# A planning margin, full-shape matmuls and single stores in a hybrid decoder step

## The chip, the cores and the metric

The kernel runs on one core of one Trainium2 chip. The metric is device time in microseconds (us), the median of three runs.

## The reference

One step of a one-layer decoder is computed for a prompt of 512 tokens and for 8 samples of 8 new tokens each, so 576 tokens in all, with model width 1024:

```python
proj = rmsnorm(x, norm1_w) @ w_in        # q, k, v, gate of retention; q, k, v of attention
ro = swish(gate) * groupnorm(retention(q, k, v, state))
ao = dilated_attention(q, k_all, v_all)  # k_all: the cached 1024 rows, then the new rows
x = x + concat([ro, ao]) @ w_out
ua, ub = split(rmsnorm(x, norm2_w) @ w_up)
x = x + (silu(causal_conv3(ua)) * ub) @ w_down
y = rmsnorm(x, normf_w)
```

Beside y, the new retention states, the windows of keys and values (cached rows followed by the new ones) and the convolution states are outputs. All data are 32-bit floats. There are eight retention heads and eight attention heads of 64 columns, handled as four head pairs (hp 0 to 3).

## The kernel before, in words

**Dense matmuls.** Every projection is cut into chunks of 128 output columns. Weights and activations are split into a high and a low part (`whi`, `wlo`; `bhi`, `blo` and others), and a chunk is 48 matmuls of 288 columns (line 254): 8 row blocks, three products, two halves of the 576 tokens. ACT makes `whi`, DVE makes `wlo`, SP loads the raw weights.

**The input projection** (`in_proj`) has 28 chunks. The first 12 feed retention, the next 12 feed attention (for each head pair: keys, queries, values), and the last 4 are the retention gates. While they run, small work is put between them: retention until 149 us, then attention until about 339 us. The output projection, the up and the down projections follow.

**Attention of the prompt** (`attn_unit`, 16 units: a head pair and a block i of 128 queries, whose scores reach over (i+1)*128 keys). For i > 0 the queries are split as well: `qa`, 128 rows high, holds the high part of one head twice, and `ql` holds the low part of both heads, one in its upper and one in its lower 64 partitions. The scores of each head are a full matmul with `qa` (line 764) and a matmul over 64 rows with half of `ql` (line 766). Then come DVE (add the bias, minimum), ACT (exponential), POOL (scale), PE transposes (line 791), copies and the product with the values (line 804).

**Attention of the samples** (`attn_sample`, 8 units: a head pair and four samples). The cached keys are transposed on PE (line 877, `keys`). A unit has scores in four column groups of 32 (line 887), softmax, transposes (lines 910 and 911, the last one only 64 columns wide), two ACT copies and one DVE copy into `spt`, and the product with the values (line 923) in four column groups: six blocks of 128 rows and one of 64 rows, which holds the new tokens.

**natural** transposes new keys and values back to token rows (line 495: four transposes of 128 columns and one of 64). `store_window` writes them out with one DMA for the prompt (line 504) and eight of 4 KB for the samples (line 507).

**The order is planned.** Each stream is a generator. `Merge` keeps a clock in ns, runs the stream that is due, and the order in which they emit is the order of the instructions on every engine. A stream yields a pair (cost, wait): the clock moves on by cost, and the stream is due again wait later. Streams with a work total (`left`: `in_proj`, `attn_prompt`, `attn_sample`) share what time is over; the others go first once they are due. The clock only fixes an order: the hardware waits on semaphores alone. `room(n)` and `give(n)` count the four PSUM tiles `m`. At most two prompt units and two sample units are under way. Two gates matter:

```python
# in_proj: keys, queries, values of hp 2 wait for all six units of hp 0, those of hp 3 for hp 1
while hp > 1 and (sec < 3 and ret_done[0] < hp - 1 or sec > 3 and used.get(hp - 2, 0) < 6):
    yield None
# attn_sample: at most six value tiles are held; the next ones load after a unit's line 923
while len(V) > 5:
    yield None
```

The tables of the functions are these:

Of the kernel before, what the change touches and what calls it, by code (L numbers as in the profile page):

```python
# [11 lines left out]
F32R = mybir.dt.float32r  # L12
# [6 lines left out]
P = 128  # L19
D = 1024  # L20
NP = 512
NS = 64
T = NP + NS
H2 = T // 2
B = 8
TS = 8
PAST = 1024
# [5 lines left out]
KEYS = 768  # L33
SK = KEYS + TS
# [61 lines left out]
class Merge:  # L96
# [6 lines left out]

    def __init__(self):
        self.clock, self.live, self.n = 0.0, [], 0

    def floor(self):
        return min([e["vt"] for e in self.live if e["left"] and not e["stuck"]], default=0.0)
# [6 lines left out]
    def run(self, until=None):  # L115
        while self.live and not (until and until()):
            free = [e for e in self.live if not e["stuck"]]
            assert free, "every stream waits"
            ok = [e for e in free if e["at"] <= self.clock]
            if ok:  # L120
                e = min(ok, key=lambda e: (e["left"] is not None, e["vt"] if e["left"] else e["at"], e["n"]))
            else:
                e = min(free, key=lambda e: (e["at"], e["n"]))
                self.clock = e["at"]
            try:
                c = next(e["g"])
            except StopIteration:
                self.live.remove(e)
                c = (0.0, 0.0)
            if c is None:  # L130
                e["stuck"] = True
                continue
            low = self.floor()
            for x in self.live:
                if x["stuck"]:
                    x["stuck"] = False
                    x["vt"] = max(x["vt"], low)
            self.clock += c[0]
            e["at"] = self.clock + c[1]
            if e["left"]:  # L140
                p = c[2] if len(c) > 2 else c[0]
                e["vt"] += p / e["left"]
                e["left"] = max(e["left"] - p, 2000.0)
# [3 lines left out]
def decoder_step(ctx, tc, a):  # L147
    nc = tc.nc
    pe, dve, act, pool, sp = nc.tensor, nc.vector, nc.scalar, nc.gpsimd, nc.sync
# [10 lines left out]
    held = [0]  # L160

    def room(n):

        while held[0] + n > 4:
            yield None
        held[0] += n

    def give(n):
        held[0] -= n

    def dtile():
        return psd.tile([P, 1024], F32, name="d", tag="d")
# [1 line left out]
    def f32(ap):  # L174
        return ap.bitcast(F32)
# [91 lines left out]
    ident = cst.tile([P, P], F32, name="ident")  # L267
# [27 lines left out]
    def rows_of(j):  # L295
        return (P, slice(j * P, (j + 1) * P)) if j < 4 else (NS, slice(NP, T))
# [31 lines left out]
    mg = Merge()  # L328
# [21 lines left out]
    for nme, n in (("conv_w", 66), ("conv_b", 22), ("norm2_w", 8), ("ret_gn_w", 4), ("ret_gn_b", 4)):  # L350
        src = a[nme]
# [134 lines left out]
    rpx = mid.enter_context(ExitStack())  # L486
    rp = rpx.enter_context(tc.tile_pool(name="ret", bufs=2, reuse_waits="tile"))

    def natural(src, dst):

        yield from room(2)
        p1, p2 = mtile(), mtile()
        for j in range(5):
            r, s = rows_of(j)
            pe.transpose((p1[:, s] if j < 4 else p2[:NS, :P]), src[:, s], ident)  # L495
        yield 550.0, 300.0
        act.copy(dst[:, 0:4], p1.rearrange("p (j c) -> p j c", j=4))
        dve.tensor_copy(dst[:NS, 4], p2[:NS, :P])
        give(2)

    def store_window(nat, which, hp):
        c = slice(hp * P, (hp + 1) * P)
        op_ = a[f"o_w{which}_p"].rearrange("a (j p) h d -> p (a j) (h d)", p=P)[:, :, c]
        sp.dma_start(op_, nat[:, 0:4])
        os_ = a[f"o_w{which}_s"]
        for b in range(B):
            sp.dma_start(os_[b, PAST:PAST + TS].rearrange("t h d -> t (h d)")[:, c], nat[b * TS:(b + 1) * TS, 4])

    copies = []
    for which in "kv":  # L510
# [10 lines left out]
    def in_post(m, ps):  # L521
        sec, hp = m // 4, m % 4
        y = tok(ps)
        if sec == 3:
            t = atp.tile([P, T], F32, name="t3", tag="t6", bufs=1)
            dve.tensor_mul(t, y, rstd_b)
            yield 0.0, 800.0
            act.activation(t, t, AF.Silu)
            yield 0.0, 1700.0
            while ret_done[0] <= hp:  # L530
                yield None
            (dve if hp == 3 else pool).tensor_tensor(roT[:, hp], roT[:, hp], t, op=OP.mult)
            ready.add(hp)
        elif sec < 4:
            while sec == 1 and hp not in kready:
                yield None
            r = R.setdefault(hp, {})
            t = rp.tile([P, T], F32, name=f"r{sec}", tag=f"r{sec}", bufs=2)
            dve.tensor_mul(t, y, kds.pop(hp) if sec == 1 else rstd_b)
            if m in first:  # L540
                evac.append(m)
            while not psm:
                yield None
            yield 0.0, 700.0
            if sec in (1, 2):
                n = rp.tile([P, 5, P], F32, name=f"n{sec}", tag=f"n{sec}", bufs=2)
                yield from natural(t, n)
                r["kv"[sec - 1]] = n
            if sec == 1 and hp < 3:
                mg.add(load_kdec(hp + 1))  # L550
            r[sec] = t
        else:
            r = A.setdefault(hp, {})
            t = atp.tile([P, T], F32, name=f"t{sec}", tag=f"t{sec}", bufs=1 if sec == 6 else 2)
            if sec == 4:
                dve.scalar_tensor_tensor(t, y, -(DH ** -0.5), rstd_b, op0=OP.mult, op1=OP.mult)
                yield 0.0, 2300.0
                for h2, q in halves():
                    pool.tensor_copy(qbs[hp % 2][q, :, h2 * TS:(h2 + 1) * TS],
                                     t[q, NP:].rearrange("p (b t) -> p b t", b=B))  # L560
            else:
                dve.tensor_mul(t, y, rstd_b)
                yield 0.0, 1700.0
                n = atp.tile([P, 5, P], F32, name=f"n{sec}", tag=f"n{sec}", bufs=1 if sec == 5 else 2)
                yield from natural(t, n)
                if sec == 6:
                    r["v"] = n
            r[sec] = t
            if sec > 4:
                yield 0.0, 3100.0  # L570
                store_window(n, "k" if sec == 5 else "v", hp)
# [159 lines left out]


    half, used = {}, {}
    pbs, O, flying = {}, {}, {"p": 0, "s": 0}

    def load_bias(hp):
        for h2 in range(2):
# [3 lines left out]
    def attn_unit(hp, i):  # L741

        n = (i + 1) * P
        S, PT = [], []
        if i:

            q_ = A[hp][4][:, i * P:(i + 1) * P]
            qa = [kvb[0].tile([P, P], F32R, name=f"qa{h2}", tag=f"qa{h2}", bufs=2) for h2 in range(2)]
            ql = kvb[0].tile([P, P], F32R, name="ql", tag="ql", bufs=2)
            for h2, q in halves():  # L750
                act.copy(qa[h2][q], q_[q])
                act.copy(qa[h2][other(h2)], q_[q])
            yield 0.0, 1000.0
            for h2, q in halves():
                dve.tensor_sub(ql[q], q_[q], f32(qa[h2][q]))
            yield 0.0, 500.0
        yield from room(2)
        pss = [mtile() for _ in halves()]
        if i == 0:
            for h2, q in halves():  # L760
                pe.matmul(pss[h2][:, :n], A[hp][4][q, :P], A[hp][5][q, :n], start=True, stop=True)
        else:
            for h2 in range(2):
                pe.matmul(pss[h2][:, :n], qa[h2], kk[hp][h2][:, :n], start=True, stop=False)  # L764
            for h2, q in halves():
                pe.matmul(pss[h2][:, :n], ql[q], kk[hp][h2][q, :n], start=False, stop=True)  # L766
        for ps in pss:
            S.append((ps, atp.tile([P, 512], F32, name="s", tag="s", bufs=4),
                      atp.tile([P, 4], F32, name="sc", tag="sc", bufs=8)))
# [43 lines left out]
                ready.add(4 + hp)  # L813
        flying["p"] -= 1

    kk, scored = {}, {}

    def k_split(hp):

# [10 lines left out]
    def other(h2):  # L830
        return slice(64 - h2 * 64, 128 - h2 * 64)
# [15 lines left out]
    kvb = []  # L847
    SW = SK + NS

    def attn_sample():  # L850
# [31 lines left out]
        def unit(u):  # L882
# [25 lines left out]
            ps = dtile()  # L908
            for j in range(6):
                pe.transpose(ps[:, j * P:(j + 1) * P], s[:, j * P:(j + 1) * P], ident)  # L910
            pe.transpose(ps[:NS, KEYS:KEYS + P], s[:, SK:], ident)
            yield 770.0, 200.0
            pt = kvb[0].tile([P, 7, P], F32, name="spt", tag="spt", bufs=1)
            dve.tensor_copy(pt[:, :3].rearrange("p j q -> p (j q)"), ps[:, :384])
            act.copy(pt[:, 3:6].rearrange("p j q -> p (j q)"), ps[:, 384:KEYS])
            act.copy(pt[:NS, 6], ps[:NS, KEYS:KEYS + P])  # L916
            yield 0.0, 2200.0
            yield from room(1)
            ps = mtile()
            for j in range(7):  # L920
                for x in range(4):
                    n, v = (P, V[u, x][:, j]) if j < 6 else (NS, A[hp]["v"][:NS, 4])
                    pe.matmul(ps[x * 32:(x + 1) * 32, :P], pt[:n, j, x * 32:(x + 1) * 32], v, start=j == 0, stop=j == 6,  # L923
                              tile_position=(0, x * 32))
                if j == 3:
                    yield 900.0, 0.0
# [68 lines left out]
    psm.append(ctx.enter_context(tc.tile_pool(name="psm", bufs=4, space=PSUM, reuse_waits="tile")))  # L995
    mg.run(lambda: fin_ret)
    rpx.close()

    kvx = mid.enter_context(ExitStack())
    kvb.append(kvx.enter_context(tc.tile_pool(name="kv", bufs=2, reuse_waits="tile")))  # L1000

    MIX = [4, 5, 6, 7, 0, 1, 2, 3]

# [8 lines left out]

    mg.add(mix_split())
    mg.run()
    mid.close()


# [306 lines left out]
```

## Time and profile before

| | |
|---|---|
| median of three runs | 831.99 us (831.43 to 834.12) |
| profiled execution | 832.6 us, span 830.8 us |
| PE busy | 813.8 us, 98% of the span |
| DVE, ACT, POOL busy | 412.5, 295.3, 148.0 us |

PE is the engine of matmuls and PEld its loads of weights, which overlap them. A matmul's duration in a row includes its way through the array, so matmuls overlap and the time that one costs is read from the start of one row to the start of the next. "Busy" therefore covers short waits as well. "idle before" in a PEld row is a stop of the in-order load stream.

### The profile page before, as it was taken

Reading aid. Unit: us, or ns where it says so; the run is one execution under the profiler, and the core shown is the slowest. Engines: PE = TensorE matmul, PEld = TensorE weight load, DVE = VectorE, ACT = ScalarE, POOL = GpSimd, SP = SyncE. Lnnn points to the kernel's source line nnn. Section 1 sums busy time; section 2 is a strip of 40 time slices with the busy share of each in tenths; the row PEclk is TensorE's granted clock in tenths of the full one; section 3 lists DMA queues with packets and bytes.
Section 4 is the critical chain, followed back from the end, with each engine's and each line's share of the span. In section 5 each row is a group of like instructions: output and inputs, shape, how many; then the busy total and the mean of one; then the engine's idle time right before and its main releaser. Section 6 shows DMA issues by size and latency. Waiting matters only on the chain.

```text
span 830.8 us, 15970 instructions
## 1 busy us (share of the span) xinstructions
PE 813.8 (98%) x6559; PEld 772.2 (93%) x6559; DVE 412.5 (50%) x792; ACT 295.3 (36%) x511; POOL 148.0 (18%) x234
## 2 busy tenths in 40 slices
PE   7999999999999999999999999999999999999995
PEld 6999999887887888999999999999999999999995
DVE  4664555665546456754545455432235545453333
ACT  5422232554446367333223323311223323342222
POOL 1321202011111113023122212100012322210111
PEclk9999999999999999999999999999999999999998
DMA  9354653658787774455265554543334445543213
GB/s 269 102 173 125 203 175 97 185 158 236 217 219 197 219 212 121 110 177 179 78 201 178 178 174 125 168 140 89 93 102 153 152 152 178 171 156 96 71 52 115
DMA packets 180247, 128.68 MB, mean 155 GB/s; under 512 B 15424, under 2 KB 176848, under 8 KB 179661
## 3 DMA queue, kind: packets, MB, share of 16 engines
q1 hardware_dynamic: 179021, 93.75, 40.3%
q10 hardware_dynamic: 928, 33.63, 11.2%
q8 instruction: 52, 0.85, 0.4%
q0 software_dynamic: 224, 0.28, 0.1%
q14 instruction: 22, 0.18, 0.1%
HBM read 121.52 MB, written 39.66 MB: 194 GB/s over the span
## 4 chain that ended last, share of the span: by engine, by line
PE 96%; ACT 1%; DVE 1%; DMA 0%; POOL 0%; issue 0%; ACTq 0%; DVEq 0%; POOLq 0%
PE d L254 75%; PE m L877 2%; PE m L923 2%; PE d L451 2%; PE m L804 1%; PE d L887 1%; PE m L791 1%; PE m L495 1%; PE px L410 1%; PE m L1214 1%; PE px L254 1%; PE m L663 1%; PE m L764 1%; PE d L910 1%; PE m L766 1%; PE m L627 1%
## 5 line engine op out<-in xcount | busy, mean ns | idle before, releaser
L219 ACT ACTIVATE whi<-wraw 128x1024 fp32r<-128x1024 f32 (+2 forms) x114 | 110.6, 970 | 364.9 <-issue 182.6
L229 DVE TENSOR_TENSOR wlo<-wraw,whi 128x1024 fp32r<-128x1024 f32 (+2 forms) x114 | 126.7, 1112 | 120.4 <-ACT whi L219 117.0
L254 PE MATMUL d<-bhi,whi 128*128 128x288 f32 x768 | 173.3, 307 | 0.0
L254 PE MATMUL d<-bhi,wlo 128*128 128x288 f32 x768 | 164.3, 295 | 0.0
L254 PE MATMUL d<-blo,whi 128*128 128x288 f32 x768 | 163.9, 295 | 0.0
L254 PE MATMUL d<-hhi,whi 128*128 128x288 f32 x704 | 150.9, 296 | 0.0
L254 PE MATMUL d<-hhi,wlo 128*128 128x288 f32 x704 | 150.8, 296 | 0.0
L254 PE MATMUL d<-hlo,whi 128*128 128x288 f32 x704 | 150.7, 296 | 0.0
L254 PEld LDWEIGHTS d<-bhi,whi 128*128 128x128 f32 x768 | 121.5, 189 | 5.2 <-issue 3.6
L254 PEld LDWEIGHTS d<-bhi,wlo 128*128 128x128 f32 x768 | 123.3, 188 | 0.0
L254 PEld LDWEIGHTS d<-blo,whi 128*128 128x128 f32 x768 | 123.2, 188 | 0.0
L254 PEld LDWEIGHTS d<-hhi,whi 128*128 128x128 f32 x704 | 113.4, 189 | 0.1
L254 PEld LDWEIGHTS d<-hhi,wlo 128*128 128x128 f32 x704 | 113.4, 189 | 0.0
L254 PEld LDWEIGHTS d<-hlo,whi 128*128 128x128 f32 x704 | 113.4, 189 | 0.0
L1122 DVE TENSOR_TENSOR ue<-d,rstd_b 128x512 f32<-128x512 f32 x22 | 15.2, 691 | 74.6 <-PE d L254 74.6
L1141 POOL TENSOR_TENSOR g<-g,cv 128x512 f32<-128x512 f32 x20 | 25.7, 1287 | 142.1 <-DVE g L1138 136.7
L785 POOL TENSOR_SCALAR s<-s,sc 128x128 f32<-128x128 f32 (+3 forms) x32 | 18.2, 575 | 141.1 <-DVE sc L783 139.9
L1038 POOL TENSOR_TENSOR acc<-acc,sq 128x576 f32<-128x576 f32 x13 | 20.9, 1607 | 104.2 <-ACT sq L1037 104.2
L1127 POOL COPY cout<-ue 128x2 f32<-128x2 f32 x22 | 5.7, 258 | 137.8 <-DVE ue L1122 137.8
L878 DVE COPY kt<-m 128x384 f32<-128x384 f32 x32 | 17.8, 556 | 22.4 <-PE m L877 21.2
L878 ACT COPY kt<-m 128x384 f32<-128x384 f32 x32 | 15.3, 477 | 38.4 <-PE m L877 36.8
L877 PE MATMUL m<-ident,kc 128*128 128x128 f32 x192 | 27.2, 277 | 0.9 <-ACT spt L916 0.9
(264 smaller groups left out, 1030.7 us busy)
## 6 DMA issues: line engine op xcount, KB each, us to landing
wraw<-in_w_up_dram SPq DMA_DIRECT2D x44, 512.0 KB
wraw<-in_w_in_dram SPq DMA_DIRECT2D x26, 512.0 KB
kc<-in_cache_win_k_dram SPq DMA_DIRECT2D x32, 256.0 KB
vc<-in_cache_win_v_dram SPq DMA_DIRECT2D x32, 256.0 KB
wraw<-in_w_down_dram SPq DMA_DIRECT2D x16, 384.0 KB
wraw<-in_w_down_dram SPq DMA_DIRECT2D x16, 320.0 KB
kc<-in_cache_win_k_dram SPq DMA_DIRECT2D x64, 64.0 KB
vc<-in_cache_win_v_dram SPq DMA_DIRECT2D x64, 64.0 KB
```

The costliest lines, as they stand in the source:

```text
L219: act.activation(split[i][0][:, c], raw[i][:, c], AF.Copy)
L229: dve.tensor_sub(lo[:, c], raw[i][:, c], f32(hi[:, c]))
L254: pe.matmul(ps[:, C0 + s * H2:C0 + (s + 1) * H2], wt[:, rows[k] if rows else k - k0], x[k][:, s * H2:(s + 1) * H2], start=first and k == k ...
L410: pe.transpose(ps[:, s], xn[:r, j, k * P:(k + 1) * P], ident[:r, :r])
L451: pe.matmul(ps[i][:, C0 + s * H2:C0 + (s + 1) * H2], wt[:, k], x[k][:, s * H2:(s + 1) * H2], start=k == 0 and wt is hi and x is xhis, stop ...
L785: pool.tensor_scalar(s[:, :n], s[:, :n], c[:, 2:3], 1.0, op0=OP.mult, op1=OP.mult)
L877: pe.transpose(ps[:, j * P:(j + 1) * P], K[u, x][:, 3 * w + j], ident)
L878: (act.copy if w else dve.tensor_copy)(kt[:, w * 384:w * 384 + 384], ps[:, :384])
L923: pe.matmul(ps[x * 32:(x + 1) * 32, :P], pt[:n, j, x * 32:(x + 1) * 32], v, start=j == 0, stop=j == 6, tile_position=(0, x * 32))
L1038: pool.tensor_tensor(acc, acc, sq, op=OP.add)
L1122: dve.tensor_mul(u[:, 2:NP + 2], ya[:, :NP], rstd_b[:, :NP])
L1141: eng.tensor_tensor(g[:, :NP], g[:, :NP], c[:, :NP], op=OP.mult)
```

## The change

The planner gets a margin of 0.8 us, in force from the end of retention to the end of attention. A stream without a work total whose wait is 0.2 us or more becomes due 0.8 us later, and a PSUM tile that is given back counts as free only 0.7 us later. The low query parts go to two fixed tiles whose other 64 partitions are zero, so line 766 becomes a full matmul; a lock lets one unit at a time hold them. The last transposes of `natural` and of a sample unit, and the last block of line 923, become 128 wide, with zeros for the rows that don't count. One ACT copy takes the place of two. The eight stores of new rows become one.

```diff
-            e["at"] = self.clock + c[1]
+            e["at"] = self.clock + c[1] + (self.margin if c[1] >= 200.0 and not e["left"] else 0.0)
...
     def room(n):
-        while held[0] + n > 4:
-            yield None
+        while True:
+            while freed and freed[0][0] <= mg.clock:
+                held[0] -= freed.pop(0)[1]
+            if held[0] + n <= 4:
+                break
+            yield (0.0, max(freed[0][0] - mg.clock, 10.0)) if freed else None
         held[0] += n
+    freed = []
     def give(n):
-        held[0] -= n
+        if mg.margin:
+            freed.append((mg.clock + 700.0, n))
+        else:
+            held[0] -= n
...
-    def natural(src, dst):
+    def natural(src, dst, rows):
...
-        for j in range(5):
-            r, s = rows_of(j)
-            pe.transpose((p1[:, s] if j < 4 else p2[:NS, :P]), src[:, s], ident)
+        for j in range(4):
+            pe.transpose(p1[:, j * P:(j + 1) * P], src[:, j * P:(j + 1) * P], ident)
+        pe.transpose(p2[:, :P], src[:, T - P:], ident)
...
-        dve.tensor_copy(dst[:NS, 4], p2[:NS, :P])
+        dve.tensor_copy(dst[rows, 4], p2[UP, :P])
...
-        for b in range(B):
-            sp.dma_start(os_[b, PAST:PAST + TS].rearrange("t h d -> t (h d)")[:, c], nat[b * TS:(b + 1) * TS, 4])
+        sp.dma_start(os_[:, PAST:PAST + TS].rearrange("b t h d -> b t (h d)")[:, :, c], nat[NS:, 4])
...
+                if sec == 6:
+                    pool.memset(n[:NS, 4], 0.0)
+                yield from natural(t, n, UP)
...
-            ql = kvb[0].tile([P, P], F32R, name="ql", tag="ql", bufs=2)
+            while flying["ql"]:
+                yield None
+            flying["ql"] = 1
...
-                dve.tensor_sub(ql[q], q_[q], f32(qa[h2][q]))
+                dve.tensor_sub(qls[h2][q], q_[q], f32(qa[h2][q]))
...
-                pe.matmul(pss[h2][:, :n], ql[q], kk[hp][h2][q, :n], start=False, stop=True)
+                pe.matmul(pss[h2][:, :n], qls[h2], kk[hp][h2][:, :n], start=False, stop=True)
+            flying["ql"] = 0
...
-            pe.transpose(ps[:NS, KEYS:KEYS + P], s[:, SK:], ident)
+            pe.transpose(ps[:, KEYS:KEYS + P], s[:, SW - P:], ident)
...
-            act.copy(pt[:, 3:6].rearrange("p j q -> p (j q)"), ps[:, 384:KEYS])
-            act.copy(pt[:NS, 6], ps[:NS, KEYS:KEYS + P])
+            act.copy(pt[:, 3:7].rearrange("p j q -> p (j q)"), ps[:, 384:KEYS + P])
...
-                    n, v = (P, V[u, x][:, j]) if j < 6 else (NS, A[hp]["v"][:NS, 4])
-                    pe.matmul(ps[x * 32:(x + 1) * 32, :P], pt[:n, j, x * 32:(x + 1) * 32], v, start=j == 0, stop=j == 6,
+                    v = V[u, x][:, j] if j < 6 else A[hp]["v"][:, 4]
+                    pe.matmul(ps[x * 32:(x + 1) * 32, :P], pt[:, j, x * 32:(x + 1) * 32], v, start=j == 0, stop=j == 6,
...
     rpx.close()
+    mg.margin = 800.0
...
+    for h2 in range(2):
+        qls.append(kvb[0].tile([P, P], F32R, name=f"ql{h2}", bufs=1))
+        pool.memset(f32(qls[h2][other(h2)]), 0.0)
...
     mg.run()
+    mg.margin = 0.0
     mid.close()
```

## Rows read from the trace of the kernel before

**Rows 1.** The page: busy time by engine, and the chain that ended last.

```profile
PE 813.8 (98%) x6559; PEld 772.2 (93%) x6559; DVE 412.5 (50%) x792; ACT 295.3 (36%) x511; POOL 148.0 (18%) x234
PE 96%; ACT 1%; DVE 1%; DMA 0%; POOL 0%; issue 0%; ACTq 0%; DVEq 0%; POOLq 0%
```

**Rows 2.** Windows: stretch, its us, busy (count) of each engine, granted clock, DMA.

```profile
360.00:380.00 20.00, 20.00 (x154) 20.00 (x153) 10.12 (x12) 7.54 (x10) 5.06 (x3) 1.00 0.50 156
...
193.80:204.00 10.20, 8.53 (x96) 6.73 (x94) 5.38 (x15) 4.52 (x13) 1.25 (x6) 0.83 0.87 247
...
199.30:202.70 3.40, 3.40 (x57) 2.64 (x58) 2.21 (x8) 1.93 (x6) 0.30 (x1) 0.50 0.79 229
```

**Rows 3.** Timeline of PE, 193.7 to 204 us: start, us, line, out<-in, form, count, idle.

```profile
193.70 0.42 PE L254 MATMUL d<-bhi,wlo 128*128 128x288 f32 x2
...
194.62 0.82 PE L910 MATMUL d<-ident,ss 128*128 128x128 f32 x6
...
196.97 0.92 PE L877 MATMUL m<-ident,kc 128*128 128x128 f32 x6 [0.88 <-ACT spt L916]
...
199.21 2.76 PE L923 MATMUL m<-vc,spt 128*32 128x128 f32 x48
...
203.99 0.51 PE L254 MATMUL d<-bhi,whi 128*128 128x288 f32 x2
```

**Rows 4.** Waits of PEld, 148 to 345 us: us in total, times, longest.

```profile
PEld m L791 <- POOL s L785: 1.8, 7, 0.4
PEld d L887 <- POOL kt L977: 1.8, 3, 1.2
PEld m L877 <- ACT spt L916: 1.1, 1, 1.1
...
PEld m L877 <- DMA kc<-in_cache_win_k_dram: 0.4, 1, 0.4
```

**Rows 5.** Timeline of PE around a score burst of 256 columns.

```profile
166.84 0.28 PE L764 MATMUL m<-kdec,qa 128*128 128x256 f32 x1
...
167.17 0.38 PE L766 MATMUL m<-kdec,ql 64*128 64x256 f32 x1
...
167.85 0.43 PE L254 MATMUL d<-blo,whi 128*128 128x288 f32 x2
```

**Rows 6.** The same around one of 512 columns.

```profile
226.82 0.39 PE L764 MATMUL m<-ka,qa 128*128 128x512 f32 x1
...
227.93 0.42 PE L254 MATMUL d<-blo,whi 128*128 128x288 f32 x2
```

**Rows 7.** Timeline of PE around line 923.

```profile
219.34 1.52 PE L923 MATMUL m<-vc,spt 128*32 128x128 f32 x48
220.79 0.42 PE L923 MATMUL m<-n,spt 64*32 64x128 f32 x8
221.14 0.76 PE L495 MATMUL m<-ident,t 128*128 128x128 f32 x5
```

**Rows 8.** Timeline of PE: a run that ends in a narrow transpose, a full run.

```profile
241.09 0.27 PE L911 MATMUL d<-ident,ss 128*64 128x128 f32 x1
241.12 0.50 PE L254 MATMUL d<-bhi,whi 128*128 128x288 f32 x2
...
246.72 0.82 PE L877 MATMUL m<-ident,kc 128*128 128x128 f32 x6
247.29 0.38 PE L254 MATMUL d<-bhi,whi 128*128 128x288 f32 x1
```

**Rows 9.** Timeline of SP: the stores of a window's new rows.

```profile
204.10 3.49 SPq L507 DMA_DIRECT2D out_dram<-n  x8
```

**Rows 10.** Timeline of PE: scores of sample unit 1; the end of attention.

```profile
188.37 0.64 PE L887 MATMUL d<-kt,qb 128*32 128x512 f32 x4
...
335.58 0.27 PE L938 MATMUL m<-ident,ob 128*128 128x128 f32 x1
...
338.88 0.42 PE L254 MATMUL d<-bhi,whi 128*128 128x288 f32 x2
```

More of the change, by code (lines that the diff above doesn't have):

```diff
@@ L105, in __init__ @@
         self.clock, self.live, self.n = 0.0, [], 0
+        self.margin = 0.0
     def floor(self):
@@ L487, in decoder_step @@
     rp = rpx.enter_context(tc.tile_pool(name="ret", bufs=2, reuse_waits="tile"))
-    def natural(src, dst):
+    UP = slice(NS, P)
+    def natural(src, dst, rows):
         yield from room(2)
         p1, p2 = mtile(), mtile()
-        for j in range(5):
-            r, s = rows_of(j)
-            pe.transpose((p1[:, s] if j < 4 else p2[:NS, :P]), src[:, s], ident)
+        for j in range(4):
+            pe.transpose(p1[:, j * P:(j + 1) * P], src[:, j * P:(j + 1) * P], ident)
+        pe.transpose(p2[:, :P], src[:, T - P:], ident)
         yield 550.0, 300.0
         act.copy(dst[:, 0:4], p1.rearrange("p (j c) -> p j c", j=4))
-        dve.tensor_copy(dst[:NS, 4], p2[:NS, :P])
+        dve.tensor_copy(dst[rows, 4], p2[UP, :P])
         give(2)
@@ L546, in in_post @@
                 n = rp.tile([P, 5, P], F32, name=f"n{sec}", tag=f"n{sec}", bufs=2)
-                yield from natural(t, n)
+                yield from natural(t, n, slice(0, NS))
                 r["kv"[sec - 1]] = n
@@ L564, in in_post @@
                 n = atp.tile([P, 5, P], F32, name=f"n{sec}", tag=f"n{sec}", bufs=1 if sec == 5 else 2)
-                yield from natural(t, n)
+                if sec == 6:
+                    pool.memset(n[:NS, 4], 0.0)
+                yield from natural(t, n, UP)
                 if sec == 6:
@@ L733, in decoder_step @@
     half, used = {}, {}
-    pbs, O, flying = {}, {}, {"p": 0, "s": 0}
+    pbs, O, flying = {}, {}, {"p": 0, "s": 0, "ql": 0}
     def load_bias(hp):
@@ L814, in attn_unit @@
         flying["p"] -= 1
-    kk, scored = {}, {}
+    kk, scored, qls = {}, {}, []
     def k_split(hp):
```

## The prediction

> **What bounds the kernel now.** I read the page first: PE is busy 98% of the span and makes up 96% of the chain that ended last [rows 1]. So whatever the other engines save counts only where PE waits for them, and an edit must take work or waits from PE itself. "Busy" covers waits, so I looked next for stretches in which PE works below its pace. The pace is plain behind attention: 154 dense matmuls of 288 columns in 20 us, 0.130 us each [rows 2], or by proportion 0.116 us for 256 columns, 0.173 for 384 and 0.231 for 512. The windows and the timeline of the attention stretch (149 to 339 us) show one bad place: from 193.8 to 204.0 us no dense matmul starts [rows 3], PE's clock is granted at 0.83 on average, and for 3.4 us of it at half, 1.2 GHz in place of 2.4 [rows 2]. That is the first gate of the input projection: the chunks of head pair 2 wait until the last sample unit of head pair 0 has emitted its line 923, which runs at 199.21 us. Last I read the waits of the weight loads: the rest of attention has small stops scattered over it, behind POOL's scaling, POOL's small copies and ACT's copies out of PSUM [rows 4].
>
> **The change part by part.**
>
> *Low query parts, line 766.* Twelve units (i = 1, 2, 3 in four head pairs) have a pair of 64-row matmuls. With 256 columns, a burst takes from 166.84 to the third dense matmul at 167.85, 1.01 us; less two dense ones (0.26) that is 0.75 us for two full matmuls, the pair and the switches of shape [rows 5]. After, it is four full matmuls without a switch: 4 × 0.116 = 0.46, a gain of 0.29. With 512 columns, the second full matmul and the pair take 227.93 − 226.82 − 0.26 = 0.85 [rows 6]; after, 3 × 0.231 = 0.69, a gain of 0.16. For 384 I take the middle, 0.22. Four head pairs: 4 × 0.67 = 2.7 us if dense work always follows. Where a burst in column groups follows, the switch is paid anyway (0.13, below); for half of the units I take that off (6 × 0.13 = 0.8), which leaves 1.9 us. Bounds: 2.7 with dense work behind all twelve, 1.1 with a tiled burst behind all.
>
> *Two 64-row matmuls do start together: both rows of the pair stand at 167.17 [rows 5].* By the Trainium skill ("TensorEngine Tiling (Array Packing)", Key Properties), tiles run independently and matmuls on different ones in parallel; by that alone the pair costs one matmul and its full-shape form two, so the edit would lose 4 × (0.116 + 0.173 + 0.231) = 2.1 us. The rows above hold the switches as well, and I go by them.
>
> *Values of the new tokens, line 923.* The 48 matmuls of six blocks (12 groups of four) take 1.45 us up to the 64-row block, that block's 8 (two groups) 0.35 us [rows 7]. With a pace g and a switch s, 12g + s = 1.45 and 2g + s = 0.35: g = 0.11, s = 0.13. After, the block runs on without the switch before it: 0.13 × 8 units = 1.0 us. Bounds: nothing, and twice that.
>
> *Narrow transposes, lines 495 and 911.* The last of a run costs 0.03 us up to the next dense matmul [rows 8], and a full run of six takes 0.57 us, which is five at 0.11 and 0.03 for the last: the same. Nothing for all 24; the upper bound is 0.08 each, 1.9 us.
>
> *ACT, DVE, POOL.* One ACT copy per sample unit less and a few small memsets on POOL: neither engine is near its limit (36% and 18% [rows 1]); dense matmuls hide them. Without that cover it would be a few tenths per unit.
>
> *Stores.* Eight issues take 3.49 us of SP [rows 9], so one in place of eight frees some 3 us, eight times over. SP issues the key loads behind them, but PE's one stop for a key load is 0.4 us [rows 4]. I take nothing; bounds 0 and 0.4.
>
> *The margin.* What it can win: in the gate's stretch line 923 itself, from 199.21 on, runs at the low clock, and 10.2 us hold some 6 us of small bursts at the paces above, so 4 us are lost there. Outside it, the first two stops of [rows 4] make 3.6 us on PEld, and I estimate the many smaller ones behind other engines at as much again, 7 us; the loads run ahead of the matmuls, so I take half, 3.5 us. The margin moves the transposes and products of a unit 0.8 us behind each step they wait for; dense matmuls go there instead. It does not move the scores of a sample unit (line 887), whose 0.6 us is a delay given at its start: their stop behind POOL (1.8 [rows 4], half of it 0.9) stays. So 2.5 us.
>
> What it can cost: between its scores and line 923 a sample unit has six waits of 0.2 us or more, so its plan grows by 6 × 0.8 = 4.8 us, plus a PSUM tile that comes free later. Line 923 lets the next value tiles load and opens the gates for head pairs 2 and 3, so dense work is held back 4.8 us longer in the plan at each gate, and the last unit ends later. On the chip the order counts, not the margin: sample unit 1 needs from 188.37 [rows 10] to 199.21 [rows 3] between scores and values, while the plan's longer stretch also receives work that stood ahead of the gate before (the last prompt unit of head pair 0). At the end, line 938 stands 3.3 us ahead of the first output projection matmul [rows 10], room for part of a shift of 4.8. Estimate: the 4 us of gate 1 stay about as they are, and gate 2 and the end together cost 0.4 us; bounds: 4 won, 14.4 lost.
>
> *Sum:* −1.9 − 1.0 − 2.5 + 0.4 = −5.0 us. The profiled execution took 832.6 (its span 830.8 and 1.8 around it), 0.6 above the median of 832.0. So 832.6 − 5.0 = 827.6, and 827.0 as a median.
>
> **The rivals.**
>
> *Gates (slower).* The margin starves PE. Three places (two gates and the end) can each lose 4.8 us: 14.4 − 1.9 − 1.0 − 2.5 = +9.0, 841 us. For it speaks that gate 1 is short of dense work already [rows 3] and that a starved stretch falls to the low clock [rows 2]; against it, that the same work is still there to be put in. From 5.4 us lost on, the gain is gone.
>
> *The margin moves waits and removes none.* What one burst wins the next loses, and only the shapes count: −2.9, 829.1 us. For it: the stops are behind POOL and ACT queues, which stay as long.
>
> *Full shapes don't pay.* The pair overlapped and now runs in sequence, the rule above: +2.1 − 1.0 − 2.5 + 0.4 = −1.0, 831 us. Against it: rows 5 and 6.
>
> *Gate 1 is cured as well.* The work moved into it fills it, and the clock stays high: −5.0 − 4.0 with the shapes at their upper bounds (−0.8 − 1.0) is −10.8, 821.2 us. For it: more work is planned there; against: the unit's chain is as long.
>
> **How the numbers follow.** Chances: the forecast 0.50, gates 0.13, waits only moved 0.18, no gain from shapes 0.08, gate cured 0.11. The forecast's own range is 824 to 829.5, from the bounds of line 766 and half of the margin's term. The range reaches from 821 (gate cured) to 834 (gates with 7 to 8 us lost) and leaves out the worse half of the gate case and little else. A measurement here can't tell a change under 0.3%, 2.5 us: faster is under 829.5, slower over 834.5. Faster takes nearly all of the forecast (0.46), the cured gate (0.11) and just over half of the moved waits (0.10): 0.67. Slower is most of the gate case, 0.12; same is the rest, 0.21.
>
> **What would show it.** Right: line 766 in 128-row form, the next dense matmul at its own pace behind it, and bursts of 0.46 us for 256 columns; one shape through line 923; smaller stops of PEld behind L785 and L916; SP with one store issue per window. Dense work should still stop once near the first gate for about 10 us. Wrong: a stretch without dense matmuls of over 15 us at a gate, a second one at half clock, or idle PE between line 938 and the output projection. Wrong too if the bursts of line 766 take as long as before.

## The result, and the profile after

The changed kernel takes 838.71 us (median of 6 runs, 837.55 to 841.39) against 832.98 us of the kernel before on the same chip: ratio 1.0082, 95% interval 1.0066 to 1.0098. It is slower, outside the forecast's range. The profiled execution took 837.55 us, 5.0 more than that of before.

The page after, busy time and the chain:

```profile
PE 810.4 (97%) x6559; PEld 774.0 (93%) x6559; DVE 412.1 (49%) x792; ACT 296.8 (36%) x505; POOL 148.2 (18%) x240
PE 94%; ACT 2%; DVE 1%; DMA 1%; issue 0%; POOL 0%; ACTq 0%; SPq 0%; POOLq 0%; DVEq 0%
```

PE lost 3 us of busy time, and its share of the chain fell from 96% to 94%. Windows of the changed kernel: the three stretches of attention without a dense matmul (at the two gates and at the end), and the time at half clock.

```profile
184.60:209.10 24.50, 18.26 (x173) 13.38 (x172) 12.14 (x35) 11.87 (x34) 2.62 (x8) 0.86 0.62 182
...
245.70:251.10 5.40, 4.65 (x80) 3.69 (x80) 3.63 (x10) 2.19 (x4) 0.00 (x0) 1.00 1.03 275
...
336.50:344.30 7.80, 6.35 (x103) 4.86 (x101) 3.92 (x9) 5.10 (x9) 1.06 (x4) 1.00 0.20 64
194.40:201.20 6.80, 5.40 (x22) 4.51 (x23) 4.18 (x13) 2.79 (x8) 1.31 (x5) 0.50 0.72 206
```

The first stretch was 10.2 us long with 1.67 us of idle PE and 3.4 us at 1.2 GHz [rows 2]; now it is 24.5 us, with 24.50 − 18.26 = 6.24 us idle and 6.8 us at 1.2 GHz. The second adds 0.75 us of idle PE, the third 1.45. Waits of the weight loads after, the two sources from which the forecast priced the margin's gain:

```profile
PEld d L904 <- POOL kt L993: 2.3, 3, 1.7
...
PEld m L808 <- POOL s L802: 1.9, 3, 1.5
```

Timeline of PE in the first stretch:

```profile
184.49 0.43 PE L265 MATMUL d<-bhi,wlo 128*128 128x288 f32 x2
...
185.51 1.51 PE L904 MATMUL d<-kt,qb 128*32 128x512 f32 x16
...
194.28 0.71 PE L777 MATMUL m<-t,t 64*128 64x128 f32 x2 [1.90 <-ACT n L510]
...
201.66 1.09 PE L821 MATMUL m<-pt,n 128*64 128x128 f32 x16
...
205.05 0.44 PE L821 MATMUL m<-pt,n 128*64 128x128 f32 x4 [1.93 <-ACT pt L812]
205.42 1.52 PE L939 MATMUL m<-vc,spt 128*32 128x128 f32 x48
...
209.05 0.43 PE L265 MATMUL d<-bhi,whi 128*128 128x288 f32 x2
```

(Line 265 is the dense line, 904 the sample scores, 939 the sample values, 821 the prompt values.) The dense work ran out at 184.5 us, 9.2 us earlier than before [rows 3], and was let in again at 209.05, 5.1 us later. Sample unit 1 starts its scores only when the dense work is gone; before, 5.3 us ahead of its end [rows 3, 10]. From these scores to its values it now takes 205.42 − 185.51 = 19.9 us, where it took 10.8 before. At the end, the last two dense matmuls of the input projection stand in the row at 336.29, the last sample unit follows alone, and the output projection begins at 344.25:

```profile
336.29 0.42 PE L265 MATMUL d<-bhi,wlo 128*128 128x288 f32 x2
...
342.04 1.52 PE L939 MATMUL m<-vc,spt 128*32 128x128 f32 x48 [0.65 <-DVE spt L931]
...
344.16 0.33 PE L954 MATMUL m<-ident,ob 128*128 128x128 f32 x1 [0.39 <-ACT ob L948]
344.25 0.52 PE L265 MATMUL d<-bhi,whi 128*128 128x288 f32 x2
```

The shapes did what the forecast said. Timeline around a burst of 256 columns and around line 939:

```profile
309.73 0.28 PE L780 MATMUL m<-kdec,qa 128*128 128x256 f32 x1
...
310.46 0.42 PE L265 MATMUL d<-blo,whi 128*128 128x288 f32 x2
```

```profile
297.93 1.52 PE L939 MATMUL m<-vc,spt 128*32 128x128 f32 x48
299.26 0.40 PE L939 MATMUL m<-n,spt 128*32 128x128 f32 x8
299.59 0.88 PE L894 MATMUL m<-ident,kc 128*128 128x128 f32 x6
```

The burst takes 310.46 − 309.73 − 0.26 = 0.47 us in place of 0.75 [rows 5] (0.46 was forecast); the values of a sample unit 1.66 us in place of 1.80 [rows 7].

### The profile page after: what moved, and what is told of

It reads as the page before. It is cut to its first block, busy times and chain, and to the rows that moved or that the text cites. A ratio compares the mean times of both kernels' runs of the same rounds, so it can differ in the third digit from the quotient of the medians.

```text
span 835.8 us, 15903 instructions
## 1 busy us (share of the span) xinstructions
PE 810.4 (97%) x6559; PEld 774.0 (93%) x6559; DVE 412.1 (49%) x792; ACT 296.8 (36%) x505; POOL 148.2 (18%) x240
## 4 chain that ended last, share of the span: by engine, by line
PE 94%; ACT 2%; DVE 1%; DMA 1%; issue 0%; POOL 0%; ACTq 0%; SPq 0%; POOLq 0%; DVEq 0%
PE d L265 74%; PE m L894 2%; PE d L462 2%; PE m L939 1%; PE d L904 1%; PE m L808 1%; PE m L821 1%; PE m L1235 1%; PE px L421 1%; PE m L507 1%; PE px L265 1%; PE m L677 1%; PE d L927 1%; PE m L780 1%; PE m L641 1%; PE m L659 1%
## 5 line engine op out<-in xcount | busy, mean ns | idle before, releaser
L802 POOL TENSOR_SCALAR s<-s,sc 128x128 f32<-128x128 f32 (+3 forms) x32 | 17.9, 569 | 150.3 <-DVE sc L800 125.0
L895 DVE COPY kt<-m 128x384 f32<-128x384 f32 x32 | 17.8, 557 | 33.0 <-PE m L894 30.1
```

What stands on the lines that cost most here:

```text
L802: pool.tensor_scalar(s[:, :n], s[:, :n], c[:, 2:3], 1.0, op0=OP.mult, op1=OP.mult)
L895: (act.copy if w else dve.tensor_copy)(kt[:, w * 384:w * 384 + 384], ps[:, :384])
```

## The experiments

Edits are against the changed kernel unless it says otherwise. "Ratio" is to the kernel before on the same chip, with its 95% interval. "First stretch" is the time between two dense matmuls at the first gate in the run's timeline (24.4 us in the changed kernel).

**1. The parts: margin, steps, tiles.**

```diff
-    mg.margin = 800.0
+    mg.margin = 0.0
```

> The changed kernel with the margin at 0: full shapes, the lock on the low query parts, the single stores and the merged copy stay. Theory (the margin holds back the sample units, dense work runs out at the gates and at the end): the loss is gone and the shapes alone show, 829 to 831 us against 833 for the kernel before, and the stretch without dense matmuls at the first gate is back to about 10 us from 24.5. Rival 1 (the lock or the full shapes cost the time): it stays at 836 us or more.

829.19 us, ratio 0.9948 (0.9931 to 0.9965); first stretch 3.4 us (about 10 was expected), no fall of the clock during attention, the output projection 0.2 us behind the input projection. The margin costs 838.7 − 829.2 = 9.5 us by the medians, 11 by the ratios (1.0082 − 0.9948 = 0.0134). **This version beats both kernels.** Windows of attention as a whole, with the margin and without:

```profile
148.80:344.30 195.50, 184.53 (x1818) 160.53 (x1816) 108.36 (x278) 104.60 (x241) 29.75 (x78) 0.98 0.67 190
```

```profile
148.80:334.50 185.70, 181.69 (x1810) 157.56 (x1809) 110.08 (x280) 101.39 (x238) 29.08 (x76) 1.00 0.70 197
```

With the margin attention takes 9.8 us longer. Idle PE makes 7.0 of it (10.97 against 4.01 us). The rest is close to what the low clock costs by an estimate: the 48 value matmuls took 2.69 us at 1.2 GHz [rows 3] and 1.45 at 2.4 [rows 7], so the 5.40 busy us at 1.2 GHz lose 2.5.

The margin alone in the kernel before (Merge, `room`, `give` and the two settings; everything else as before):

> The kernel before with the margin alone (steps and PSUM tiles), its small shapes, eight stores and free low query tiles as they were. Theory: slower than the changed kernel by what the shapes save, 840 to 844 us, with a stretch of 20 us or more without dense matmuls at the first gate. Rival 1 (lock or shapes cost the time): 829 to 833 us.

845.54 us, 1.0151 (1.0111 to 1.0190), a little above the expected range; first stretch 25.6 us. The loss needs neither the lock nor the shapes.

```diff
-        if mg.margin:
+        if False:                 # give(): tiles free at once, steps keep the margin
```

> The changed kernel with the margin on the steps alone; a PSUM tile counts as free at once when it is given back. Theory in its first form (six waits of a sample unit, 4.8 us each): most of the loss is here, 836 to 838 us. Rival 2 (the later tiles hold back the key transposes and bursts): little of it, 830 to 833 us.

```diff
-            e["at"] = self.clock + c[1] + (self.margin if ... else 0.0)
+            e["at"] = self.clock + c[1] + 0.0    # tiles alone
```

> The changed kernel with the later PSUM tiles alone; no step is due later. Theory in its first form: near the kernel with no margin, 830 to 833 us, first gate about 12 us. Rival 2 (the tiles): 836 to 838 us, first gate over 18 us.

Steps alone 839.99 us, 1.0074 (1.0046 to 1.0102), first stretch 24.2 us; tiles alone 841.46 us, 1.0094 (1.0068 to 1.0121), 18.9 us. Each half costs as much as both, and both times lie above all ranges expected. The first form of the theory, six waits of 0.8 us per sample unit, doesn't explain the tiles at all: the expectation for them failed.

**2. Which streams.** Steps alone, without or only for sample units:

```diff
+ ... if c[1] >= 200.0 and not e["left"] and e["g"].__name__ != "unit" else 0.0)
+ ... if c[1] >= 200.0 and e["g"].__name__ == "unit" else 0.0)
```

> As the run with the margin on the steps alone (840 us), but the sample units have none; the prompt units and the streams behind the projection keep it. Theory of the chain of the sample unit: near the kernel with no margin, 829 to 833 us, first gate under 12 us. Rival 3 (the prompt units hold the gate, since their four units count for it as well): 837 us or more.

> The complement: the margin on the steps of the sample units alone. Theory of the chain of the sample unit: most of the loss, 836 to 840 us, first gate over 18 us. Rival 3: 829 to 833 us.

Without them 832.53 us, 0.9989 (0.9973 to 1.0005), first stretch 7.9 us; on them alone 845.86 us, 1.0140 (1.0108 to 1.0171), above the expected range, first stretch 17.9 us and 12.1 us at the second gate. The steps cost mainly through the sample units: the others' steps cost 832.5 − 829.2 = 3.3 us. The parts don't add up: the sample units' steps alone cost 16.7 us, all steps together 10.8.

**3. More dense work at the gate.** Two chunks of retention gates moved from the end to before head pair 2 (the edit shown); and only the first of them, without a margin:

```diff
-    IN_ORDER += [4 * sec + hp for hp in range(4) for sec in (5, 4, 6)]
-    IN_ORDER += [12 + hp for hp in range(4)]
+    IN_ORDER += [4 * sec + hp for hp in range(2) for sec in (5, 4, 6)] + [12, 13]
+    IN_ORDER += [4 * sec + hp for hp in range(2, 4) for sec in (5, 4, 6)] + [14, 15]
```

> The changed kernel with its full margin; two of the four chunks of retention gates (head pairs 0 and 1), which wait for nothing in attention, are moved from the end of the input projection to just before the gate for head pair 2. Theory (the loss is a lack of dense work at the first gate): the stretch without dense matmuls there falls from 24.4 us to 12 us or less and no fall of the clock is left in it; the time falls by 4 to 8 us to 830 to 835 us, unless the end, now with 12.6 us less dense work, loses as much. Rival (the loss is in the waits themselves, wherever the dense work stands): it stays at 837 us or more with the same idle time of PE, about 11 us.

> No margin, and one chunk of retention gates moved to just before the gate for head pair 2. With no margin that gate lost almost nothing (3.4 us without dense matmuls, clock high), so theory: same as with no margin, 828 to 830 us. If the stop is still worth something: up to 2 us less.

With the margin 847.77 us, 1.0155 (1.0130 to 1.0181): **the time got worse by 9 us, and the theory as it stood fell.** The first gate is cured; windows of this run at the second gate and at the end:

```profile
249.80:263.70 13.90, 11.04 (x119) 8.26 (x118) 7.46 (x25) 7.75 (x22) 0.73 (x2) 0.88 0.68 191
323.90:354.00 30.10, 20.07 (x222) 14.38 (x220) 11.89 (x35) 13.85 (x33) 4.13 (x12) 0.89 0.23 64
```

The hole moved: 13.9 us at gate 2, and 30.1 us at the end with 10 us of idle PE. Without a margin the moved chunk costs too: 832.19 us, 0.9986 (0.9971 to 1.0002), where 828 to 830 was expected. So a lack of dense work at the gate is not the whole of it; it looks as if something serial sets the end of attention, and dense work decides where the hole shows. The candidate is the series of sample units: scores, softmax, values; only then do value tiles come free, and the keys of the next unit wait for those. In the groups by line, first and last start of the values (line 939), with no margin and in the changed kernel:

```profile
L939 PE MATMUL m<-vc,spt x384: 272/273/298, 176.9 to 327.2; 128*32 128x128 f32 x192
```

```profile
L939 PE MATMUL m<-vc,spt x384: 272/273/297, 181.0 to 343.3; 128*32 128x128 f32 x192
```

The series takes 150.3 us without a margin and 162.3 in the changed kernel. With its later start (4.1 us) it ends 16.1 us later, and the time is 9.5 us longer: without a margin dense work still ran for some 7 us behind the last values, until 334.5, and that room is used up first.

**4. The link cut.** Values are loaded by a stream of their own, so that keys don't wait for value tiles:

```diff
                 ahead(4 * u + x + 4, "k")
-                while len(V) > 5:
-                    yield None
-                ahead(4 * u + x + 1, "v")
+                keyed[0] += 1
...
+        def values():
+            for n in range(32):
+                while len(V) > 5 or keyed[0] <= n:
+                    yield None
+                ahead(n + 1, "v")
+                came[divmod(n, 4)] = mg.clock
+                yield 0.0, 100.0
```

and a unit waits before line 939 until its last value tile was asked for 7 us ago.

> The changed kernel with its full margin, but the value tiles of the samples are loaded by a stream of their own: the key transposes of the next unit no longer wait for the value products (line 939) of the present one, and a unit waits for its values just before these products. New theory (the eight sample units stand in series, scores, softmax, values, then the next keys, and the margin lengthens each of the seven links by 2 us or more, which sets the end of attention): without the link the margin costs little, 829 to 833 us, and the stretches without dense matmuls are under 10 us. Rival (the margin costs through its stops, whatever the order of the units): it stays at 837 us or more.

> The same with the margin at 0. New theory: the series has some slack without a margin, so little is left to win: 827 to 830 us, against 829.2 with no margin alone.

With the full margin 837.32 us, 1.0052 (1.0032 to 1.0071); with none 831.24 us, 0.9979 (0.9967 to 0.9990), 2 us more than with the link. **Both expectations failed:** the full margin still costs 6.1 us without the link, and its time lies in the rival's range. For the full margin the cut is worth 1.4 us by the medians, 2.5 by the ratios. The end is cured (0.1 us between the two projections), but the first stretch is still 21.4 us. Window and timeline of it in the run with the full margin:

```profile
187.20:208.60 21.40, 17.31 (x179) 11.93 (x177) 14.67 (x45) 11.50 (x29) 2.56 (x8) 1.00 0.76 224
```

```profile
197.59 1.52 PE L944 MATMUL m<-vc,spt 128*32 128x128 f32 x48
...
207.53 1.09 PE L821 MATMUL m<-pt,n 128*64 128x128 f32 x16
208.56 0.40 PE L265 MATMUL d<-bhi,whi 128*128 128x288 f32 x1
```

The sample values (line 944 here) now run 11 us ahead of the dense work; the gate opens behind the prompt's fourth unit (16 matmuls of line 821). Each half of the margin without the link:

> Keys free of the value tiles as in the run with free keys (837.3 us), the margin on the steps alone, no later PSUM tiles. If the link of the sample units is how the steps cost (840.0 us with the link): 830 to 834 us, first gate under 12 us. If the steps cost through their chain at the gate itself, link or not: 836 us or more.

> Keys free of the value tiles, the later PSUM tiles alone, no margin on the steps. If the later tiles cost by holding back the keys inside the series (841.5 us with the link): 830 to 834 us. If they cost by themselves, at every burst that asks for two tiles: 837 us or more.

Steps 833.90 us, 0.9998 (0.9985 to 1.0011), against 839.99 with the link; tiles 834.17 us, 0.9997 (0.9980 to 1.0015), against 841.46. **The link is worth 6 to 7 us to either half by itself**, and the tiles cost as the steps do, inside the series. Both times stand at the upper end of what was expected. The first stretches stay long (17.7 and 19.4 us, where under 12 was expected of the steps). Window of the stretch with the tiles alone (that of the steps alone stands at the end of this text):

```profile
187.90:207.40 19.50, 15.91 (x158) 11.61 (x157) 11.84 (x37) 12.02 (x35) 3.51 (x11) 0.91 0.82 228
```

PE is idle in them for 2.7 us (steps), 3.6 us (tiles) and 4.1 us (both); against no margin without the link these runs lose 2.7, 2.9 and 6.1 us. So without the link idle PE at the first gate is about as large as what either half still loses, and two thirds of what both lose; the length of a stretch by itself says little.

**5. Half the margin** (400 on the steps, 350 on the tiles):

> The changed kernel with half the margin: 400 ns on the steps, 350 ns on the tiles. If the loss follows the length of the chains: about half of it, 832 to 836 us. If it comes from a threshold in the order: near one end, 829 or 839 us.

836.28 us, 1.0024 (1.0013 to 1.0035): 7.1 of 9.5 us by the medians, 0.0076 of 0.0134 by the ratios; the median lies just above the expected range. The loss lies between the ends, so it is not one jump between no margin and the full one; one point doesn't show its shape.

**6. The stores.** No margin, eight stores; the same eight issued by POOL; and the single store alone in the kernel before.

```diff
-        sp.dma_start(os_[:, PAST:PAST + TS].rearrange("b t h d -> b t (h d)")[:, :, c], nat[NS:, 4])
+        for b in range(B):
+            sp.dma_start(os_[b, PAST:PAST + TS].rearrange("t h d -> t (h d)")[:, c],   # second run: pool
+                         nat[NS + b * TS:NS + (b + 1) * TS, 4])
```

> No margin; the single store is undone, eight stores of 4 KB per window. By the forecast's term (nothing, bound 0.4 us): 829.2 to 829.6 us. If SP's issues hold attention back: 831 us or more.

> No margin, eight stores per window as in the run of 836.2 us, but issued from the queue of POOL, not SP. If the eight stores cost because their issues stand in front of the key loads on SP: back to 829 to 831 us, and no wait of PE for a key load. If it is the eight transfers themselves: it stays at 835 us or more.

> The kernel before with the single store alone, nothing else of the change. PE waited 0.4 us for a key load there, so if a store's price is only what PE waits for loads: same as before, 0 to 1 us faster. If SP's time costs in any order as it did with the full shapes: about 7 us faster, 826 us.

Eight on SP 836.24 us, 1.0042 (1.0027 to 1.0057), 7.0 more than with the single store though PE's matmuls run in the same order; eight on POOL 830.49 us, 0.9945 (0.9925 to 0.9965). The price is SP's time at these stores, not the transfers. Waits during attention with eight stores on SP, PE's and SP's own:

```profile
PE m L895 <- DMA kc<-in_cache_win_k_dram: 5.2, 3, 2.3
```

```profile
SPq L520 <- DMA wraw<-in_w_in_dram: 4.9, 6, 1.3
SPq L520 <- DMA out_dram<-n: 4.5, 6, 1.7
```

PE's wait is missing with the single store and with the eight on POOL. SP's rows say that its time at the eight stores (line 520) is in part a wait for earlier transfers. This run is also slower than the kernel before, by about 3 us, although that has the eight stores too, and the small shapes. The single store alone in the kernel before: 830.75 us, 0.9960 (0.9945 to 0.9975), 3.4 us, where 0 to 1 or 7 were expected. Timeline of that run at the first gate (line 876 is the key transposes):

```profile
194.60 0.71 PE L495 MATMUL m<-ident,t 128*128 128x128 f32 x5
195.14 0.82 PE L876 MATMUL m<-ident,kc 128*128 128x128 f32 x6
```

The stop of 0.88 us in front of these transposes, which the row of before puts down to ACT's copy [rows 3], is gone with the stores, and so is the fall of the clock; the first stretch is 8.0 us. PE's order is that of before, and the copy's second half (line 915 there) starts only after these transposes have begun, so they did not need it:

```profile
195.82 0.26 ACT L915 COPY spt<-d 64x128 f32<-64x128 f32 x1
```

That the stop of before was a wait for a key load is inferred; no row of before names it.

**7. The shapes.** No margin; pairs of 64-row matmuls again, and the 64-row block again (in the second run the product takes the same rows of `pt`, cut here):

```diff
-                pe.matmul(pss[h2][:, :n], qls[h2], kk[hp][h2][:, :n], start=False, stop=True)
+                pe.matmul(pss[h2][:, :n], qls[h2][q], kk[hp][h2][q, :n], start=False, stop=True)
...
-                    v = V[u, x][:, j] if j < 6 else A[hp]["v"][:, 4]
+                    k, v = (slice(0, P), V[u, x][:, j]) if j < 6 else (UP, A[hp]["v"][UP, 4])   # second run
```

> No margin; line 766 back to its pairs of 64-row matmuls (the fixed low query tiles and the lock stay). By the forecast's term the full shapes are worth 1.9 us (bounds 1.1 and 2.7): 830.3 to 831.9 us against 829.2. By the rule of tiles that run in parallel, 2.1 us faster: 827.

> No margin; the block of new tokens in line 939 back to 64 rows (the upper 64 partitions), everything else as with no margin. By the forecast's term it costs 1.0 us (bounds 0 and 2): 830.2 us against 829.2, relative to the kernel before 0.9960 against 0.9948.

Pairs 830.75 us, 0.9972 (0.9961 to 0.9984): full shapes are worth 1.6 us by the medians, 2.0 by the ratios. Block 830.58 us, 0.9963 (0.9950 to 0.9976): 1.4 and 1.2 us.

## Why the prediction was wrong, point by point

- **Line 766 and line 923** (−1.9 and −1.0): right, 1.6 to 2.0 and 1.2 to 1.4 us. The Trainium skill ("TensorEngine Tiling (Array Packing)", Key Properties) says that tiles run in parallel; the two rows of a pair that start together [rows 5] agree. By that alone the pairs would have been 2.1 us faster; the run shows that it is not the whole price. The same section says that a change of tiling mode drains the engine. The 0.13 us per switch that the forecast worked out [rows 7] fits: the values of a sample unit lost 1.80 − 1.66 = 0.14 us, one switch. No row shows a drain by itself.
- **The stores** (nothing, bound 0.4 us): wrong. I read the one row that names a key load [rows 4]. A second stop stood under ACT's name, and it went with the stores: they cost 3.4 us in the order of before, 7.0 us in that of no margin, where PE waits 5.2 us for keys by name.
- **The margin's gain** (2.5 us): it did not come. It starts from two waits of 1.8 us [rows 4]. The one behind POOL's scaling, which the margin should shorten, is 1.9 us after; the one behind POOL's small copies, which it should leave, is 2.3. With everything else equal the margin costs 9.5 us, where 2.5 − 0.4 = 2.1 us of gain were forecast.
- **The step that failed** is "the 4 us of gate 1 stay about as they are, and gate 2 and the end together cost 0.4 us". I priced the longer chain once per gate and let the work that is moved fill it. The runs showed otherwise: gate 1 went from 1.67 us of idle PE and 3.4 us at 1.2 GHz to 6.24 and 6.8, gate 2 and the end lost 0.75 and 1.45 us of idle PE. Two things were left out. Dense work, freed of the delayed steps, runs ahead and is gone 9.2 us earlier, while unit 1 takes 9.1 us longer from scores to values, not the plan's 4.8. And the units stand in series: their values take 12.0 us longer from first to last than without a margin. The link through the value tiles is one part of that series, and either half of the margin costs 6 to 7 us through it; with both halves the cut gives back only 1.4 to 2.5 us.
- **The rival "Gates"** was the right one in its kind (841 us; 838.7 measured), at a chance of 0.13. That its number came so close is in part luck: its picture, three holes that each lose 4.8 us, was not right. The holes lost unequally, and the runs under 3 closed the first hole and lost more at the others; and the sum had no term for the stores.
- **Open:** with the link cut both halves together still cost 837.3 − 831.2 = 6.1 us, each alone about 2.8. What holds the first gate there was not tested; that the prompt's fourth unit opens it is read from a timeline. The lock on the low query tiles was not run by itself. With no margin it is the only part of the change that the planner sees, and the order of PE's matmuls in its trace is not that of before. The shapes and the store, 1.6, 1.4 and 3.4 us by their own runs, together win only 4.3 us, and with eight stores this kernel is 3 us slower than before. So the order that the lock brings probably takes some of the gain back, the more the busier SP is.

## What to carry to other kernels

A delay in a planned order can be paid for along a serial chain of units, and not only at the place where it is put in: find which buffers make the next unit wait for the present one, count the links, and only then price the margin. Here more filler at the hole moved the hole. Leaving the steps of the chain undelayed removed 7.5 of the 10.8 us that the steps cost; cutting one link removed most of the cost of either half, and little of that of both. Instructions of an issuing queue can have a price even if the trace names almost no wait for it: here the row of 0.4 us [rows 4] stood for stores that cost 3.4.

## What was not expected of the hardware

A store of 64 pieces of 512 bytes is one issue of 0.67 us on SP, where the eight issues of one window took 3.49 us [rows 9]; from POOL's queue the eight cost attention nothing that could be measured (830.5 against 829.2 us). Groups of SP's stores of new rows after the change:

```profile
L519 SPq DMA_DIRECT2D out_dram<-n x8: 671/674/751, 136.9 to 302.0; - x8
```

In the changed kernel's first stretch PE's clock stood at 1.2 GHz for 6.8 of 24.50 us; it fell at 194.4, right behind a stop of PE of 1.90 us (the row at 194.28). It stayed at 2.4 GHz in another stretch that was as free of dense matmuls: in the run with free keys and steps alone, PE is busy 14.97 of 17.70 us, its longest stop is 0.69 us, and the granted clock is 1.00. No run tests what decides it. Window of that stretch, and the row of the stop:

```profile
187.50:205.20 17.70, 14.97 (x168) 10.26 (x166) 11.72 (x34) 9.90 (x26) 3.54 (x8) 1.00 0.77 223
```

```profile
196.30 0.74 PE L895 MATMUL m<-ident,kc 128*128 128x128 f32 x3 [0.69 <-ACT ka L842]
```
